# Two gates of a linear recurrence: from two 128-row products to pairs of 64-row tiles of the matmul array

## The chip, the cores and the metric

The kernel runs as one program on one core of one Trainium2 chip. The metric is the device time of one execution in microseconds (us). The core has five engines that run side by side and wait for each other by semaphores: PE (TensorE, matmuls), DVE (VectorE), ACT (ScalarE), POOL (GpSimd) and SP (SyncE, which here issues most DMAs).

## The reference

The program is one decoder block on 512 tokens of width 1024. A first norm and a wide projection feed a pooling mixer and a gated linear recurrence; both are merged by sigmoid gates, projected out, normed again and sent through a mixture of 16 experts, two per token. What matters here is the recurrence:

```python
xc = conv(u) + conv_b                                  # causal, 4 taps, per channel
xh = xc.reshape(b_, s_, LRU_HEADS, LRU_HEAD_DIM)       # 16 heads of 64 channels
r = sigmoid(einsum('bshc,hcd->bshd', xh, w_r) + b_r)   # a 64x64 matrix per head
i = sigmoid(einsum('bshc,hcd->bshd', xh, w_i) + b_i)   # another 64x64 matrix per head
log_a = -RG_C * r * softplus(-lam)
a = exp(log_a)
bt = sqrt(-expm1(2.0 * log_a)) * (i * xc)
h[t] = a[t] * h[t-1] + bt[t]                           # along the 512 tokens
y_b = (h * gelu(gate_in)) @ proj_b
```

## The kernel before, in words

Activations lie feature-major: 128 channels on the partitions, 512 tokens along a row. A block `c` of 128 channels, of which there are 8, so holds two heads. Products are computed to near float32 precision by splitting each operand into a high and a low part of type float32r; one product is then three matmuls (high by high, high by low, low by high: `mm3`, lines 241 to 244). Weights arrive in chunks of 1 MB (`raw`), and each half of a chunk is split by one ACT cast (line 151, `w` high) and one DVE subtraction (line 152, `w` low). The program calls them `w6_0`, `w6_1` and so on: chunk 6, first and second half.

The stages around the change follow each other on PE:

- **Recurrence input**: for each `c` a product of 24 matmuls (`zl`), an ACT and three DVE instructions for the convolution (`xc`, lines 286 to 289), and its split `xcp` (ACT line 291, DVE line 292). The gates of block `c` are computed two blocks later: `lru_gates` (line 295) multiplies `xcp` by two matrices of 128x128, each of which holds the 64x64 matrices of two heads on its diagonal and zeros beside them, into the PSUM banks `pr` and `pi`. ACT evicts each bank with one sigmoid (lines 300 and 302) and goes on with a tanh (304) and an exp (307).
- **Pooling input** (`zp`, 4 products), with running sums on DVE (`pn`, `pz`) and a split `zp`; the last two gate blocks are computed here.
- **Gate input** (`zg`, 8 products, from chunks 6 to 9). Beside it ACT and DVE do the rest of the recurrence: square, sqrt, products, eight scans (line 317), gelu and the splits `yh` and `yl`.
- **Merge** (`zga` and `ya`), and all that follows.

Three things set the order of the work. The instructions of each engine stand in a fixed order, which a scheduler chose when the program was built from its own estimate of when each would be ready; a scheduler's choice can so put a weight split early or late among other work. Tiles come from pools with a fixed number of buffers (`b8`: 20 buffers of 16 KB a partition, `s4`: 6 of 4 KB a partition, PSUM: 8 banks), and who takes a buffer waits until it is free. Weight loads are issued in one order on SP's queue, at most three in flight. ACT evaluates some functions only with the right table loaded (`ACT_TABLE_LOAD`): sigmoid and exp as they are used here need different ones.

The block-diagonal matrices are built at the start: DVE clears `bd_raw` (line 199), four DMAs write the 64x64 matrices, and one ACT cast and one DVE subtraction of 2048 elements a partition split it into `bd0` and `bd1`.

Of the kernel before, what the change touches and what calls it, by code (L numbers as in the profile page):

```python
# [8 lines left out]
F32 = mybir.dt.float32  # L9
F32R = mybir.dt.float32r  # L10
# [3 lines left out]
AF = mybir.ActivationFunctionType  # L14
# [3 lines left out]
P = 128  # L18
S = 512
D = 1024  # L20
KD = D // P
# [15 lines left out]
def tile_hybrid_block(  # L37
# [7 lines left out]
    PE, ACT, DVE, POOL, SP = nc.tensor, nc.scalar, nc.vector, nc.gpsimd, nc.sync  # L45
# [7 lines left out]
    const = ctx.enter_context(tc.tile_pool(name="const", bufs=1))  # L53
# [3 lines left out]
    def b8(shape, dtype, name):  # L57
        return sb.tile(shape, dtype, tag="b8", name=name, bufs=20)

    def s4(shape, dtype, name):  # L60
        return sb.tile(shape, dtype, tag="s4", name=name, bufs=6)
# [4 lines left out]
    def bank(name):  # L66
        return psum.tile([P, 512], F32, tag="ps", name=name)
# [4 lines left out]
    class Feat:  # L72
        """[P, KD, S] in two tiles."""

# [19 lines left out]

# [1 line left out]
    chunks = []  # L96
# [36 lines left out]
    raws, pairs, loads = {}, {}, {}  # L133
# [16 lines left out]
    def split(r, hi, lo):  # L150
        ACT.copy(hi, r)  # L151
        DVE.tensor_tensor(lo, r, hi.bitcast(F32), op=ALU.subtract)  # L152
# [17 lines left out]

# [1 line left out]
    x_rows = [s4([P, D], F32, f"x_rows{t}") for t in range(NT)]  # L172
# [7 lines left out]

# [1 line left out]
    ident = const.tile([P, P], F32, name="ident")  # L182
# [10 lines left out]
    for nm, ap, n in vecs:  # L193
# [3 lines left out]
        r0 += n  # L197
    bd_raw = b8([P, 2, KD, P], F32, "bd_raw")
    DVE.memset(bd_raw, 0.0)
    for j, w in enumerate((rg_w_r, rg_w_i)):  # L200
        wv = w.rearrange("(c two) k m -> two k c m", two=2)
        for two in range(2):
            half = slice(64 * two, 64 * two + 64)
            SP.dma_start(bd_raw[half, j, :, half], wv[two])
    load_raw(2)
    g1, lam, cb, br, bi, psc, g2f = (par[n] for n in ("g1", "lam", "cb", "br", "bi", "psc", "g2f"))
    cw = par["cw"].rearrange("p (j c) -> p j c", j=4)

# [1 line left out]
    def rstd_of(src, name):  # L210
# [30 lines left out]
    def mm3(acc, whi, wlo, mhi, mlo, first, last):  # L241
        PE.matmul(acc, whi, mhi, start=first, stop=False)
        PE.matmul(acc, whi, mlo, start=False, stop=False)
        PE.matmul(acc, wlo, mhi, start=False, stop=last)
# [7 lines left out]

# [1 line left out]
    sp8 = const.tile([P, KD], F32, name="sp8")  # L254
# [24 lines left out]

# [1 line left out]
    ra, ix, uu = Lazy(F32, "ra"), Lazy(F32, "ix"), Lazy(F32, "uu")  # L281
    bd = []

    def lru_conv(c, ps):
# [8 lines left out]
        return c, xc, xp  # L293

    def lru_gates(c, xc, xp):
        pr = bank(f"pr{c}")
        mm3(pr, bd[0][:, 0, c, :], bd[1][:, 0, c, :], xp[:, 0], xp[:, 1], True, True)
        pi = bank(f"pi{c}")
        mm3(pi, bd[0][:, 1, c, :], bd[1][:, 1, c, :], xp[:, 0], xp[:, 1], True, True)
        ACT.activation(ra[c], pr, AF.Sigmoid, bias=br[:, c:c + 1])  # L300
        it = s2([P, S], F32, f"it{c}")
        ACT.activation(it, pi, AF.Sigmoid, bias=bi[:, c:c + 1])
        DVE.tensor_tensor(ix[c], it, xc, op=ALU.mult)
        ACT.activation(uu[c], ra[c], AF.Tanh, scale=sp8[:, c:c + 1])
# [9 lines left out]
    def lru_scan(c):  # L314
        ACT.activation(uu[c], uu[c], AF.Sqrt)
        DVE.tensor_tensor(ix[c], uu[c], ix[c], op=ALU.mult)
        DVE.tensor_tensor_scan(uu[c], ra[c], ix[c], 0.0, op0=ALU.mult, op1=ALU.add)

    pend = []
    for c in range(KD):  # L320
        wp = weights(c_lru[c // 2], 2, 3)
        ps = feat_block(wp, (c % 2) * P, KD, xh, xl, f"zl{c}")
        if c == 0:
            with tc.issue_after(xl_last):
                softplus()
            bd += [b8([P, 2, KD, P], F32R, f"bd{i}") for i in range(2)]
            split(bd_raw, *bd)
        if len(pend) == 2:
            lru_gates(*pend.pop(0))
        pend.append(lru_conv(c, ps))  # L330

# [1 line left out]
    icnt = const.tile([P, PAD], F32, name="icnt")  # L333
# [74 lines left out]

# [1 line left out]
    m = Lazy(F32, "m")  # L410
# [17 lines left out]

# [1 line left out]
    NR = 2 * NG + NE  # L430
# [53 lines left out]
    rows = const.tile([P, NE], I32, name="rows")  # L484
# [13 lines left out]

# [1 line left out]
    x2s, h2s, xts, xpart, xg = {}, {}, {}, [], []  # L500
# [160 lines left out]
    for t in range(NT):  # L661
# [4 lines left out]
        for n in range(2):  # L666
            po = bank(f"po{t}_{n}")
            for kh in range(2):
                w = weights(c_wo[n][kh], 2 if n + kh < 2 else 0, RA[2 * t + n])
                for kk in range(4):  # L670
# [6 lines left out]
                    if kk % 2 == 1:  # L677
# [3 lines left out]
                        if step == 5 and t == NT - 1:  # L681
                            xg.append(s4([P, D], F32, "xg0"))
                            POOL.memset(xg[0], 0.0)
                            first = gather(rows0, xg[0], (NT - 1) * P)
# [95 lines left out]

# [1 line left out]
    cn = bank("cn")  # L782
# [8 lines left out]
    for e in range(NE):  # L791
        pg = bank(f"pg{e}")
# [25 lines left out]

# [1 line left out]
    n_max = nc.values_load(nmi[0:1, 0:1], min_val=0, max_val=S)  # L820
# [54 lines left out]

# [1 line left out]
    xb = [b8([P, 2, D], F32, f"xb{i}") for i in range(2)]  # L877
# [73 lines left out]
```

## Time and profile before

| | |
|---|---|
| time, median of 3 runs | 697.42 us (696.87 to 699.47) |
| span of the profiled execution, first to last instruction | 695.7 us |
| median less that span | 1.7 us |
| busy: PE, DVE, ACT | 650.9, 502.5, 431.4 us |

The profiler gives the profiled execution's span and no separate time for it, so the 1.7 us by which the median of the runs exceeds the span stand for what lies around it and for the difference between executions. Matmuls are pipelined: a matmul's row lasts 0.39 us, but the next one starts 0.23 us after it, so PE reads as busy all the time when they follow each other without a gap. A wait is printed at the end of a row, in brackets, as idle time of the engine and what ended it.

### The profile page before, as it was taken

What the parts mean: (1) busy time and instruction counts of PE and PEld (TensorE: products, weight loads), DVE (VectorE), ACT (ScalarE), POOL (GpSimd) and SP (SyncE); (2) the same over time, 40 slices, a digit from 0 to 9 for tenths busy, and PEclk for the clock granted to TensorE, in tenths of its full rate; (3) what the DMA queues carried; (4) which work ended last, traced back from release to release, by engine and by line L of the source; (5) the groups of instructions that cost most, each with busy time, mean ns of one, the idle gap of its engine ahead of it and who ended that gap; (6) DMA issues with size and microseconds to landing.
All of it is one profiled execution on the core that took longest, in us unless ns stands there. A gap on an engine that the chain in (4) does not pass through costs nothing. (4 is left out here: it accounts for less than half of the span.)

```text
span 695.7 us, 8405 instructions
## 1 busy us (share of the span) xinstructions
PE 650.9 (94%) x3044; PEld 526.8 (76%) x3044; DVE 502.5 (72%) x792; ACT 431.4 (62%) x579; POOL 79.6 (11%) x101
## 2 busy tenths in 40 slices
PE   5999999999999999999959999999999999999970
PEld 4888888788888888887747787777777777777850
DVE  6886699952322227556687898898899888887946
ACT  6599957752213225141244888888888888777913
POOL 3000000000100000000131111111111111101013
PEclk9999999999999999999988999999999999999996
DMA  7920323213217113696584999999999999999134
GB/s 215 345 79 20 127 81 118 95 62 122 65 62 241 53 69 121 235 389 236 198 310 134 334 333 342 341 351 338 331 337 336 361 336 342 335 339 365 53 98 161
DMA packets 88053, 153.23 MB, mean 220 GB/s; under 512 B 7250, under 2 KB 29894, under 8 KB 88009
## 3 DMA queue, kind: packets, MB, share of 16 engines
q1 hardware_dynamic: 81736, 138.98, 57.5%
q0 software_dynamic: 5824, 12.64, 6.8%
q10 hardware_dynamic: 448, 1.05, 0.4%
q8 instruction: 24, 0.39, 0.2%
q14 instruction: 21, 0.16, 0.1%
HBM read 146.67 MB, written 14.16 MB: 231 GB/s over the span
## 5 line engine op out<-in xcount | busy, mean ns | idle before, releaser
L152 DVE TENSOR_TENSOR w<-raw,w 128x1024 fp32r<-128x1024 f32 x248 | 293.6, 1220 | 69.7 <-ACT w L151 67.6
L151 ACT CAST w<-raw 128x1024 fp32r<-128x1024 f32 x248 | 249.7, 1051 | 59.4 <-DVE w L152 14.1
L727 PE MATMUL pu<-w,xt 128*128 128x512 f32 x128 | 51.9, 406 | 2.3 <-DVE w L152 2.3
L726 PE MATMUL pu<-w,xt 128*128 128x512 f32 x128 | 52.2, 408 | 1.8 <-ACT w L151 1.8
L726 PE MATMUL pg<-w,xt 128*128 128x512 f32 x128 | 52.8, 412 | 1.1
L727 PE MATMUL py<-w,ht 128*128 128x512 f32 x128 | 51.6, 403 | 0.0
L728 PE MATMUL py<-w,ht 128*128 128x512 f32 x128 | 50.7, 396 | 0.6 <-DVE ht L505 0.6
L728 PE MATMUL pg<-w,xt 128*128 128x512 f32 x128 | 50.4, 394 | 0.5 <-DVE xt L505 0.5
L728 PE MATMUL pu<-w,xt 128*128 128x512 f32 x128 | 50.7, 396 | 0.0
L727 PE MATMUL pg<-w,xt 128*128 128x512 f32 x128 | 50.3, 393 | 0.3 <-DVE w L152 0.3
L508 POOL DMA_INDIRECT xg<-h_rows,rows x16 | 26.9, 1679 | 197.6 <-PE xtp L718 177.8
L726 PE MATMUL py<-w,ht 128*128 128x512 f32 x128 | 48.8, 395 | 0.8 <-ACT ht L504 0.8
L743 POOL DMA_INDIRECT x_acc<-y,rows x15 | 24.6, 1639 | 62.9 <-ACT y L774 36.4
L727 PEld LDWEIGHTS pu<-w,xt 128*128 128x128 f32 x128 | 24.5, 191 | 8.8 <-DVE w L152 3.2
L726 PEld LDWEIGHTS pg<-w,xt 128*128 128x128 f32 x128 | 24.1, 188 | 9.4 <-ACT w L151 5.3
L726 PEld LDWEIGHTS pu<-w,xt 128*128 128x128 f32 x128 | 24.3, 190 | 7.7 <-ACT w L151 3.1
L726 PEld LDWEIGHTS py<-w,ht 128*128 128x128 f32 x128 | 24.5, 191 | 6.1 <-ACT ht L504 1.0
L505 DVE TENSOR_TENSOR xt<-xtp,xt 128x512 fp32r<-128x512 f32 x30 | 19.4, 686 | 13.4 <-ACT xt L504 13.4
L727 PEld LDWEIGHTS pg<-w,xt 128*128 128x128 f32 x128 | 24.1, 188 | 6.2 <-DVE w L152 0.7
L728 PEld LDWEIGHTS py<-w,ht 128*128 128x128 f32 x128 | 24.4, 191 | 5.7 <-DVE ht L505 1.0
L728 PEld LDWEIGHTS pg<-w,xt 128*128 128x128 f32 x128 | 24.0, 188 | 5.8 <-DVE xt L505 1.1
L728 PEld LDWEIGHTS pu<-w,xt 128*128 128x128 f32 x128 | 24.5, 191 | 4.8
(292 smaller groups left out, 1414.6 us busy)
## 6 DMA issues: line engine op xcount, KB each, us to landing
raw<-in_exp_w_gate_dram SPq DMA_DIRECT2D x32, 1024.0 KB, 8.0
raw<-in_exp_w_up_dram SPq DMA_DIRECT2D x32, 1024.0 KB, 7.9
raw<-in_exp_w_down_dram SPq DMA_DIRECT2D x32, 1024.0 KB, 10.7
raw<-in_w_in_dram SPq DMA_DIRECT2D x17, 1024.0 KB, 7.7
raw<-in_proj_b_dram SPq DMA_DIRECT2D x4, 1024.0 KB, 9.3
raw<-in_w_out_dram SPq DMA_DIRECT2D x4, 1024.0 KB
x_rows<-in_x_dram SPq DMA_DIRECT2D x4, 512.0 KB
xrow<-in_x_dram SPq DMA_DIRECT2D x4, 512.0 KB
```

What stands on the lines that cost most here:

```text
L151: ACT.copy(hi, r)
L152: DVE.tensor_tensor(lo, r, hi.bitcast(F32), op=ALU.subtract)
L505: DVE.tensor_tensor(lo, tv, hi.bitcast(F32), op=ALU.subtract)
L508: return POOL.indirect_dma_start(out=dst, out_offset=None, in_=h2d[:n, :], in_offset=bass.IndirectOffsetOnAxis(ap=idx, axis=0), bounds_che ...
L726: PE.matmul(ps, hi, w[:, 0, k % 2, :], start=first and k == 0, stop=False)
L727: PE.matmul(ps, hi, w[:, 1, k % 2, :], start=False, stop=False)
L728: PE.matmul(ps, lo, w[:, 0, k % 2, :], start=False, stop=last and k == 3)
L743: POOL.indirect_dma_start(out=xd, out_offset=bass.IndirectOffsetOnAxis(ap=idx, axis=0), in_=src, in_offset=None, bounds_check=S - 1, oob_i ...
```

## The change

For each head, `r` and `i` matrices now stand side by side as one matrix of 64 rows and 128 columns. The two heads of a block use the two halves of the array's rows: rows 0 to 63 write to one PSUM bank (`pg0`), rows 64 to 127 to another (`pg1`). The number of matmul instructions per block stays six (three parts for each of two heads), each with 64 rows in place of 128. In one bank lie `r` of a head and `i` of the same head in different partition halves, and the second head has the halves exchanged, so that `r` always stands in the partitions where it is used; `i` is moved to the other half by its eviction. Each sigmoid so becomes two of 64 partitions. The raw matrices lose their zeros and half their size: they move from pool `b8` to pool `s4`, the clearing goes, the split shrinks from 2048 to 1024 elements a partition, and both parts share one buffer. Two small copies build a bias with exchanged halves (`bisw`).

```diff
-    bd_raw = b8([P, 2, KD, P], F32, "bd_raw")
-    DVE.memset(bd_raw, 0.0)
+    bd_raw = s4([P, KD, P], F32, "bd_raw")
     for j, w in enumerate((rg_w_r, rg_w_i)):
         wv = w.rearrange("(c two) k m -> two k c m", two=2)
         for two in range(2):
-            half = slice(64 * two, 64 * two + 64)
-            SP.dma_start(bd_raw[half, j, :, half], wv[two])
+            jj = j ^ two
+            SP.dma_start(bd_raw[64 * two:64 * two + 64, :, 64 * jj:64 * jj + 64], wv[two])
...
+    HALVES = (slice(0, 64), slice(64, P))
+
     def lru_gates(c, xc, xp):
-        pr = bank(f"pr{c}")
-        mm3(pr, bd[0][:, 0, c, :], bd[1][:, 0, c, :], xp[:, 0], xp[:, 1], True, True)
-        pi = bank(f"pi{c}")
-        mm3(pi, bd[0][:, 1, c, :], bd[1][:, 1, c, :], xp[:, 0], xp[:, 1], True, True)
-        ACT.activation(ra[c], pr, AF.Sigmoid, bias=br[:, c:c + 1])
+        pg = [bank(f"pg{c}_{j}") for j in range(2)]
+        for w, m in ((0, 0), (0, 1), (1, 0)):
+            for j, h in enumerate(HALVES):
+                PE.matmul(pg[j], bd[w][h, c, :], xp[h, m], start=w + m == 0, stop=w == 1)
         it = s2([P, S], F32, f"it{c}")
-        ACT.activation(it, pi, AF.Sigmoid, bias=bi[:, c:c + 1])
+        for j, h in enumerate(HALVES):
+            o = HALVES[1 - j]
+            ACT.activation(ra[c][h], pg[j][h], AF.Sigmoid, bias=br[h, c:c + 1])
+            ACT.activation(it[h], pg[j][o], AF.Sigmoid, bias=bisw[o, c:c + 1])
         DVE.tensor_tensor(ix[c], it, xc, op=ALU.mult)
...
-            bd += [b8([P, 2, KD, P], F32R, f"bd{i}") for i in range(2)]
+            bdp = b8([P, 2, KD, P], F32R, "bdp")
+            bd += [bdp[:, i] for i in range(2)]
             split(bd_raw, *bd)
+            for h, o in ((HALVES[0], HALVES[1]), (HALVES[1], HALVES[0])):
+                DVE.tensor_copy(bisw[h], bi[o])
```

The scheduler moves other work in answer. PE's order stays as it was apart from the gate matmuls themselves, and so does the order of SP and of POOL. ACT and DVE change between the first recurrence block and the middle of the gate input; before and behind that they keep their order.

ACT, gates of blocks 2 and 3, before (`pr`, `pi`: gate banks; `nsp8`: the exp's scale; `sp8`: the tanh's):

```order
L307 ACT_TABLE_LOAD
L307 ACTIVATE ra0_372<-ra0_372,nsp8_214 128x512 x2
L300 ACT_TABLE_LOAD
L300 ACTIVATE ra0_372<-pr2_467,vec_90 128x512
L291 CAST xcp3_431<-xc3_426 128x512
L302 ACTIVATE it2_476<-pi2_471,vec_90 128x512
L304 ACTIVATE uu0_378<-ra0_372,sp8_213 128x512
L286 ACTIVATE xc4_480<-zl4_442,vec_90 128x512
L307 ACT_TABLE_LOAD
L307 ACTIVATE ra0_372<-ra0_372,nsp8_214 128x512
L300 ACT_TABLE_LOAD
L300 ACTIVATE ra0_372<-pr3_513,vec_90 128x512
```

ACT at the same place in the changed program, from the cast of `xcp3` on:

```order
L290 CAST xcp3_436<-xc3_431 128x512
L305 ACT_TABLE_LOAD
L305 ACTIVATE ra0_374<-pg2_0_472,vec_90 64x512
L306 ACTIVATE it2_480<-pg2_0_472,bisw_214 64x512
L305 ACTIVATE ra0_374<-pg2_1_473,vec_90 64x512
L306 ACTIVATE it2_480<-pg2_1_473,bisw_214 64x512
L308 ACTIVATE uu0_381<-ra0_374,sp8_212 128x512
L285 ACTIVATE xc4_487<-zl4_447,vec_90 128x512
L305 ACTIVATE ra0_374<-pg3_0_520,vec_90 64x512
L306 ACTIVATE it3_528<-pg3_0_520,bisw_214 64x512
L305 ACTIVATE ra0_374<-pg3_1_521,vec_90 64x512
L306 ACTIVATE it3_528<-pg3_1_521,bisw_214 64x512
```

Each block now has four sigmoids in place of two, and two blocks stand behind one table load where each had its own, because fewer exps are put between them. From the cast of `xcp1` to the copy `pu1` of the second pooling block ACT had 12 table loads, 16 sigmoids and 7 exps; it now has 7 table loads, 32 half sigmoids and 4 exps, and the same casts, copies, convolutions and tanhs.

DVE, second and third pooling group, before (`pn`, `pz`: running sums; `zp1`: the low part of the second group's split; `w7`: the weights of the gate input's second chunk):

```order
L361 TENSOR_TENSOR phead_1_767<-pn1_2_763,icnt_637 128x3
L152 TENSOR_TENSOR w7_0_875<-raw7_540,w7_0_875 128x1024
L362 TENSOR_TENSOR pz1_765<-phead_1_767,pu1_758 128x3
L152 TENSOR_TENSOR w7_1_878<-raw7_540,w7_1_878 128x1024
L365 TENSOR_TENSOR zp1_770<-pz1_765,zp1_770 128x512
L355 TENSOR_TENSOR pn2_1_809<-pu2_806 128x527
L355 TENSOR_TENSOR pn2_2_811<-pn2_1_809 128x525
L355 TENSOR_TENSOR pn2_4_813<-pn2_2_811 128x521
```

DVE at the same place in the changed program:

```order
L369 TENSOR_TENSOR phead_1_784<-pn1_2_780,icnt_650 128x3
L370 TENSOR_TENSOR pz1_782<-phead_1_784,pu1_775 128x3
L373 TENSOR_TENSOR zp1_787<-pz1_782,zp1_787 128x512
L363 TENSOR_TENSOR pn2_1_826<-pu2_823 128x527
L363 TENSOR_TENSOR pn2_2_828<-pn2_1_826 128x525
L363 TENSOR_TENSOR pn2_4_830<-pn2_2_828 128x521
L152 TENSOR_TENSOR w7_0_892<-raw7_549,w7_0_892 128x1024
L367 SCALAR_TENSOR_TENSOR pz2_832<-pn2_4_830,pu2_823 128x512
L369 TENSOR_TENSOR phead_2_834<-pn2_4_830,icnt_650 128x7
L152 TENSOR_TENSOR w7_1_895<-raw7_549,w7_1_895 128x1024
```

The two splits of `w7` stood ahead of `zp1` and now stand behind it. From `zp1` to the split `w9_0` of the gate input's last chunk DVE's queue holds these two more and otherwise the same instructions, some of them in another order.

## Rows read from the trace of the kernel before

**Rows 1.** The page's first line.

```profile
span 695.7 us, 8405 instructions
```

**Rows 2.** Chain of gate matmuls, PE timeline: start, us, engine, line, operation, out<-in.

```profile
33.47 0.39 PE L242 MATMUL pr<-xcp,bd 128*128 128x512 f32 x1
...
34.83 0.39 PE L242 MATMUL zl<-xh,w 128*128 128x512 f32 x1
```

**Rows 3.** One of six groups of gate matmuls, by tile: duration min/median/max, starts.

```profile
L242 PE MATMUL pr<-xcp,bd x8: 388/389/389, 33.5 to 81.1; 128*128 128x512 f32 x8
```

**Rows 4.** PE timeline around a 64-row product of the router (L556, L557).

```profile
312.32 0.39 PE L676 MATMUL po<-w,mt 128*128 128x512 f32 x1
312.63 0.40 PE L556 MATMUL lgt<-sel,ls 64*128 64x24 f32 x2
...
313.19 0.50 PE L674 MATMUL po<-w,mt 128*128 128x512 f32 x1
313.52 0.39 PE L675 MATMUL po<-w,mt 128*128 128x512 f32 x1
```

**Rows 5.** Busy time by stretch: length, PE, PEld, DVE, ACT, POOL, clock, DMA, GB/s.

```profile
40.00:60.00 20.00, 20.00 (x90) 16.53 (x90) 14.34 (x20) 19.86 (x27) 0.00 (x0) 1.00 0.16 54
60.00:80.00 20.00, 20.00 (x90) 16.57 (x89) 13.30 (x17) 19.84 (x25) 1.04 (x3) 1.00 0.20 66
100.00:120.00 20.00, 20.00 (x90) 16.44 (x89) 19.72 (x28) 17.33 (x26) 0.54 (x1) 1.00 0.30 95
120.00:140.00 20.00, 18.27 (x81) 14.82 (x80) 19.65 (x27) 14.52 (x20) 0.00 (x0) 1.00 0.35 116
140.00:160.00 20.00, 20.00 (x90) 16.57 (x89) 11.58 (x13) 9.99 (x12) 0.00 (x0) 1.00 0.15 54
```

**Rows 6.** PE timeline, the wait in the gate input.

```profile
131.40 0.50 PE L244 MATMUL zg<-xh,w 128*128 128x512 f32 x1 [1.73 <-DVE w L152]
```

**Rows 7.** DVE timeline, from the second pooling group to that wait.

```profile
91.59 1.22 DVE L152 TENSOR_TENSOR w<-raw,w 128x1024 fp32r<-128x1024 f32 x1
92.73 0.69 DVE L365 TENSOR_TENSOR zp<-pz,zp 128x512 fp32r<-128x512 f32 x1
...
97.20 0.69 DVE L365 TENSOR_TENSOR zp<-pz,zp 128x512 fp32r<-128x512 f32 x1 [0.68 <-ACT zp L364]
...
130.12 2.35 DVE L152 TENSOR_TENSOR w<-raw,w 128x1024 fp32r<-128x1024 f32 x2
```

**Rows 8.** ACT timeline, first gate block and second pooling group.

```profile
35.15 0.62 ACT L291 CAST xcp<-xc 128x512 fp32r<-128x512 f32 x1 [5.37 <-DVE sacc L272]
...
37.09 0.69 ACT L300 ACTIVATE ra<-pr,vec 128x512 f32<-128x512 f32 x1
37.67 0.68 ACT L302 ACTIVATE it<-pi,vec 128x512 f32<-128x512 f32 x1
...
87.43 0.58 ACT L348 COPY pu<-zp 128x512 f32<-128x512 f32 x1
```

**Rows 9.** ACT groups from 30 to 140 us: busy, mean ns, idle before.

```profile
L300 ACT ACT_TABLE_LOAD x6 | 7.7, 1283 | 0.1
...
L307 ACT ACTIVATE ra<-ra,nsp 128x512 f32<-128x512 f32 x8 | 5.7, 722 | 0.1
...
L348 ACT COPY pu<-zp 128x512 f32<-128x512 f32 x4 | 2.3, 581 | 0.0
```

**Rows 10.** An ACT copy of half the partitions (router, L553).

```profile
L553 ACT COPY ls<-lg x3: 365/366/367, 310.3 to 343.1; 64x256 f32<-64x256 f32 x3
```

**Rows 11.** The split of the gate matrices, DVE.

```profile
L152 DVE TENSOR_TENSOR bd<-bd_raw,bd x1: 2283/2283/2283, 27.4 to 27.4; 128x2048 fp32r<-128x2048 f32 x1
```

**Rows 12.** Two later stretches, columns as in rows 5.

```profile
358.00:363.00 5.00, 0.69 (x9) 0.63 (x10) 4.96 (x8) 1.31 (x2) 2.97 (x2) 0.71 1.03 385
623.00:627.00 4.00, 4.00 (x12) 3.12 (x11) 3.41 (x3) 3.04 (x3) 0.00 (x0) 0.58 1.06 337
```

**Rows 13.** Waits of SP's queue: in all, times, longest.

```profile
SPq L143 <- PE po L676: 20.4, 5, 9.9
```

More of the change, by code (lines that the diff above doesn't have):

```diff
@@ L317, in lru_scan @@
         DVE.tensor_tensor_scan(uu[c], ra[c], ix[c], 0.0, op0=ALU.mult, op1=ALU.add)
+    bisw = const.tile([P, KD], F32, name="bisw")
     pend = []
```

## The prediction

> **What bounds the kernel now.** I read the busy times by stretch first, then the idle times printed in the timelines of PE, DVE and ACT. From 40 to 80 us, where the gates are computed, PE is busy 20.00 of 20 us and ACT 19.86 and 19.84 [rows 5]: PE is the bound, and ACT has nothing to spare. From 100 to 140 us DVE is the full one, 19.72 and 19.65 of 20 [rows 5], and there PE has its only wait of the whole front part: at 131.40 us, idle for 1.73 us until DVE has split `w9_0`, weights of the gate input's last chunk [rows 6]. That split starts at 130.12, in a DVE queue that has run from `zp1` at 92.73 with one longer hole, 0.68 us at 97.20 [rows 7]. From 140 us on PE is full again and DVE and ACT half empty [rows 5]. So the reader is to see a relay: PE sets the pace to about 129 us, then DVE hands `w9_0` over late, and then PE sets the pace once more. A microsecond that PE saves before 129 us is worth nothing unless `w9_0` comes sooner as well; a microsecond by which `w9_0` comes later is paid in full. What is late or early at 140 us is taken through to the end: the later weight loads wait for buffers that matmuls free (SP's queue waits for `po`, for one, five times, 20.4 us) [rows 13].
>
> **PE's part.** A block's six gate matmuls take from 33.47 to 34.83, 1.36 us, 0.227 each [rows 2]; there are 48 of them, six groups of eight [rows 3], 10.9 us. If the two heads of a pair run side by side, a block takes three such steps, 0.68 us, and 8 blocks save 5.4 us; if they run one behind the other, nothing. No row shows two row halves at work at once, so both ends stand. I take the side-by-side value, since the two matmuls of a pair read different rows and write different banks. Going to 64 rows and back has a row, though: around the router's 64-row product the step into it is 0.31 us (312.32 to 312.63) and the first step behind it 0.33 (313.19 to 313.52) [rows 4], against 0.227; 0.08 and 0.10 more, 0.19 a block, 1.5 us for 8. PE's gain is then 5.4 - 1.5 = 3.9 us, between -1.5 and 5.4.
>
> The Trainium skill speaks on both ends. By "TensorE: Matmul & The Clock Gate", section "Part 3: Packing small matmuls — row/col tiling", matmuls in distinct row groups run concurrently; no run here shows it yet, and by it the 5.4 us stand. By "TensorEngine Tiling (Array Packing)", section "Tiling Modes", changing the tiling mode drains TensorE; rows 4 agree that a change costs, 0.08 to 0.10 us each way. If a drain were the whole rest of a matmul, 0.389 - 0.227 = 0.16 us, 16 changes would cost 2.6 us and PE's gain would be 2.8.
>
> **ACT's part.** A sigmoid of 64 partitions costs what one of 128 does: a copy of 64x256 takes 366 ns [rows 10] and one of 128x512 581 [rows 9], so a row's length of 256 more costs 215 ns, 0.84 ns an element, which leaves about 150 ns for either, whatever the partitions. Sigmoids follow each other by 37.67 - 37.09 = 0.58 us [rows 8]. Between the cast of `xcp1` at 35.15 and the copy `pu1` at 87.43 [rows 8] the changed queue has 16 more sigmoids, +9.3 us; 5 fewer table loads of 1.28 [rows 9], -6.4; 3 fewer exps of 0.72 less 0.1 overlap [rows 9], -1.9. Sum: +1.0 us. ACT is full there [rows 5], so this counts. The start comes earlier: ACT waits 5.37 us for DVE before `xcp1` [rows 8], and DVE's queue ahead of that loses half of the 2.28 us split [rows 11], -1.1, and gains two copies of 8 columns, about 0.15 each, +0.3. So `pu1` comes at 87.43 + 1.0 - 0.8 = 87.6. The removed clearing lies in the first microseconds, while DVE waits for the input, and is worth nothing; the `b8` buffers set free let loads start sooner that nobody waits for (DMA moves only 54 and 66 GB/s there [rows 5]).
>
> **DVE's part, on which the end rests.** In the changed queue the running sums behind `pu1` need not wait for the two `w7` splits: copy 0.6, two sums and `pz1` 2.1, the fix of its head 0.3 give 90.6; ACT's cast follows behind a table load and two exps (87.6 + 0.5 + 1.3 + 1.2 = 90.6) and takes 0.6; DVE starts `zp1` at about 91.5, against 92.73 [rows 7], 1.2 us sooner. But the `w7` splits now stand behind it, at 92.73 - 91.59 = 1.14 us each [rows 7], 2.3 us, in the stretch where DVE is full. Everything else from there to `w9_0` is the same work. `w9_0` is ready 2.3 - 1.2 = 1.1 us later than before. Bounds: if `zp1` starts when it did, 2.3 later; if the hole of 0.68 us closes and PE's earlier products draw ACT forward by another 1.7, 1.3 us earlier.
>
> **The sum.** PE gets to `w9_0` 3.9 us sooner and leaves it 1.1 us later; the gain turns into a wait there (and part of it at the chunk before, whose splits come later by the same). What the path gets is +1.1 us: the median of 697.42 becomes 698.5, or on the profiled execution, 695.7 [rows 1] + 1.1 = 696.8 us of span plus the 1.7 us by which the median stands above it. Own range 696.1 to 699.7. The Trainium skill has this in general: by "TensorEngine Tiling (Array Packing)", section "Performance Considerations", tiling speeds up TensorE but not PSUM evacuation; rows 5 agree, with ACT at 19.8 of 20 us.
>
> **The rivals.**
>
> *The wait brings the slower clock.* PE's waits in the gate input would add up to 1.7 + 3.9 + 1.1 = 6.7 us, close to each other. In the stretch 358 to 363 us, where PE is busy 0.69 of 5 us, the granted clock falls from its full 2.4 to a mean of 0.71 of it [rows 12], that is, to 1.2 GHz for part of it; at 623 to 627, a stretch at 0.58, 12 matmuls start in 4.00 us where 17.6 would at 0.227 [rows 12], 5.6 lost, 1.3 us. Against it: the present wait of 1.73 us left the clock at 1.00 [rows 5]. Time: 698.5 + 1.3 = 699.8 for one such stretch, 701.1 for two.
>
> *The halves don't run side by side (slower).* If they run one behind the other and the weights of a pair are not loaded ahead, each matmul takes its whole 0.389 us [rows 3] in place of 0.227: 6 x 0.16 + 0.19 = 1.16 us more a block, 9.3 us. PE has 1.7 us to spare at `w9_0` [rows 6], and 1.1 more by DVE's lateness; ACT would not be late for it. From 2.8 us on, 0.35 a block, PE decides, and 9.3 - 1.7 = 7.6 us are paid: 705.0. If they only run one behind the other at 0.227, the price is the 1.5 us of the switches, under the 2.8, and nothing shows in the end. For it: no row has such a pair. Against it: different rows, different banks.
>
> *DVE comes early (faster).* If `zp1` starts as much sooner as PE is ahead, 3.9 us, and ACT lets it, `w9_0` comes 3.9 - 2.3 = 1.6 us sooner, and with the hole closed 2.3; were the splits of `w7` then also hidden, all 3.9 to 5.4 us would come through: 693.5 to 692.0. Against it: ACT has 1.0 us more to do, not less, and stood at 19.8 of 20.
>
> **How the numbers follow.** My forecast 47%, the slower clock on top 33%, one behind the other 13%, DVE early 7%. The likeliest gives 698.5. Its own range and the clock's (697.4 to 701.0 for one stretch) are taken in, with half a microsecond below and 1.0 above for a second stretch and the difference between executions (three runs lay between 696.87 and 699.47): 695.6 to 702.0, which leaves out the last two rivals' ends. About 0.5%, 3.5 us, is what a measurement can tell from no change. Slower by more (over 700.9): 0.12 from the second rival and a quarter of the clock's, 0.20 in all. Faster by more (under 693.9): 0.06. The same: 0.74.
>
> **What would show it.** Right: six gate matmuls in about 0.9 us from the first of a block to the next `zl`; half sigmoids 0.58 us apart; ACT full from 40 to 88 us; PE idle before `zg` matmuls for 5 us or more in all, ended by `w` L152 or L151; the first `zga` about 1.1 us later than before. Wrong: a block of 1.4 us or more (second rival); fewer than 3 us of PE waits in the gate input and the first `zga` 2 us or more sooner than before (third); a stretch of the clock below 1.00 between 120 and 145 us (first). Wrong in its ground would be a loss or gain that arises behind 150 us, where both programs have the same order.

## The result, and the profile after

The changed kernel takes 705.38 us (median of four runs, 703.18 to 707.09) against 697.9 for the kernel before (median of four): a ratio of 1.0114, 95% interval 1.0092 to 1.0137. It is slower by 7.5 us, outside the range forecast. In the profiled execution the span grew by 7.8 us, and 7.4 of them are there before the merge begins: the first `zga` stands at 149.40 us in place of 141.96.

The page's first line of the kernel after, against [rows 1]:

```profile
span 703.5 us, 8424 instructions
```

The PE timeline after (start, us, engine, line, operation, out<-in; idle before and what ended it): the first gate block, against [rows 2], the wait for a later block, the waits in the gate input, against [rows 6], and the first merge matmul.

```profile
33.25 0.39 PE L243 MATMUL zl<-xh,w 128*128 128x512 f32 x1
33.57 0.96 PE L301 MATMUL pg<-xcp,bdp 64*128 64x512 f32 x6
34.46 0.50 PE L241 MATMUL zl<-xh,w 128*128 128x512 f32 x1
34.80 0.40 PE L242 MATMUL zl<-xl,w 128*128 128x512 f32 x1
...
61.80 0.50 PE L301 MATMUL pg<-xcp,bdp 64*128 64x512 f32 x2 [1.94 <-ACT xcp L290]
...
133.72 0.50 PE L241 MATMUL zg<-xh,w 128*128 128x512 f32 x1 [2.11 <-ACT w L151]
...
136.14 0.80 PE L243 MATMUL zg<-xh,w 128*128 128x512 f32 x1 [1.69 <-DVE w L152]
...
149.40 0.39 PE L241 MATMUL zga<-xh,w 128*128 128x512 f32 x1
```

The row halves do run side by side: six matmuls take from 33.57 to 34.46, 0.89 us, where they took 1.36 [rows 2]. But TensorE now waits 1.94 us for a cast on ACT in the gate stage, where it had no wait, and twice in the gate input, 3.8 us against 1.73 [rows 6].

Busy time by stretch after (columns as in [rows 5], whose stretches the rows from 40 us answer):

```profile
40.00:60.00 20.00, 19.86 (x91) 14.74 (x90) 14.17 (x18) 19.67 (x27) 0.00 (x0) 1.00 0.10 33
60.00:80.00 20.00, 17.98 (x75) 13.20 (x76) 13.14 (x18) 19.70 (x27) 0.97 (x3) 0.91 0.20 66
...
100.00:120.00 20.00, 20.00 (x89) 16.46 (x88) 19.18 (x31) 14.99 (x24) 0.00 (x0) 1.00 0.23 80
120.00:140.00 20.00, 16.05 (x61) 12.22 (x60) 19.72 (x26) 16.41 (x23) 0.54 (x1) 0.88 0.27 93
140.00:160.00 20.00, 20.00 (x85) 16.43 (x85) 12.08 (x13) 10.67 (x14) 0.00 (x0) 0.95 0.29 91
...
62.00:67.00 5.00, 4.78 (x16) 3.28 (x15) 3.40 (x5) 4.94 (x7) 0.00 (x0) 0.66 0.00 0
135.00:142.00 7.00, 5.86 (x14) 4.65 (x15) 6.66 (x9) 6.07 (x9) 0.00 (x0) 0.51 0.45 147
```

ACT is as full as it was, since there is always more for it to do. What is new is the granted clock: 0.66 from 62 to 67 us, behind the wait for the cast, and 0.51 from 135 to 142, behind those of the gate input. Both are 1.00 before.

The ACT timeline after: the first block's four sigmoids, a half sigmoid behind a whole activation, the late cast, and `pu1`, against [rows 8]; and the cast of `w9_0`.

```profile
36.96 0.68 ACT L305 ACTIVATE ra<-pg,vec 64x512 f32<-64x512 f32 x1
37.66 0.69 ACT L306 ACTIVATE it<-pg,bisw 64x512 f32<-64x512 f32 x1
38.37 0.69 ACT L305 ACTIVATE ra<-pg,vec 64x512 f32<-64x512 f32 x1
39.08 0.68 ACT L306 ACTIVATE it<-pg,bisw 64x512 f32<-64x512 f32 x1
39.78 0.78 ACT L285 ACTIVATE xc<-zl,vec 128x512 f32<-128x512 f32 x1
...
57.04 0.76 ACT L285 ACTIVATE xc<-zl,vec 128x512 f32<-128x512 f32 x1
57.70 0.68 ACT L305 ACTIVATE ra<-pg,vec 64x512 f32<-64x512 f32 x1
...
61.15 0.60 ACT L290 CAST xcp<-xc 128x512 fp32r<-128x512 f32 x1
...
91.92 0.56 ACT L356 COPY pu<-zp 128x512 f32<-128x512 f32 x1
...
132.63 1.04 ACT L151 CAST w<-raw 128x1024 fp32r<-128x1024 f32 x1
```

Each half lasts as long as a whole one, but the next starts 0.70 to 0.71 us later, behind its end; whole ones follow each other by 0.58 [rows 8], a tenth before the end of the one ahead. The half at 57.70 does start a tenth before the end of the whole activation ahead of it; more on that under e5. And `pu1` comes at 91.92, 4.5 us later.

What DVE waits for between 34 and 100 us: first before, then after (waited for, us in total, times, longest).

```profile
DVE xcp L292 <- ACT xcp L291: 8.9, 5, 2.2
...
DVE ix L303 <- ACT it L302: 1.9, 1, 1.9
```

```profile
DVE ix L307 <- ACT it L306: 14.2, 8, 3.4
DVE xc L287 <- ACT xc L285: 2.2, 3, 0.7
```

All in all 15.8 us of such waits became 19.6, and they changed place: DVE's queue now stands still at each block's product `ix`, eight times, for the last of four half sigmoids. `zp1` and the splits of `w9` further on in that queue, against [rows 7]:

```profile
95.78 0.69 DVE L373 TENSOR_TENSOR zp<-pz,zp 128x512 fp32r<-128x512 f32 x1 [0.69 <-ACT zp L372]
...
134.88 1.21 DVE L152 TENSOR_TENSOR w<-raw,w 128x1024 fp32r<-128x1024 f32 x1
...
136.62 1.21 DVE L152 TENSOR_TENSOR w<-raw,w 128x1024 fp32r<-128x1024 f32 x1
```

The loss is then two terms. `w9_0` is split from 134.88 instead of 130.12 on, 4.76 us later. From that split to the first `zga` it takes 14.52 us instead of 11.84, 2.68 more, the stretch at half clock lying there. Together 7.44, the delay of `zga`. The wait and the slow clock near 62 us cost nothing on their own, since TensorE has to wait for `w9_0` in any case (e1, below, has no wait there, and its split comes as late). ACT's cast of `w9_0` ended at 133.67, only 1.2 us ahead of DVE's split, and the first of TensorE's two waits is for it; a DVE early by more than that would have found the cast late.

### The profile page after: what moved, and what is told of

It is laid out like the page before. It is cut to its first block, busy times and chain, and to the rows that moved or that the text cites. A ratio compares the mean times of both kernels' runs of the same rounds, so it can differ in the third digit from the quotient of the medians.

```text
span 703.5 us, 8424 instructions
## 1 busy us (share of the span) xinstructions
PE 653.8 (93%) x3044; PEld 523.5 (74%) x3044; DVE 501.2 (71%) x793; ACT 440.9 (63%) x593; POOL 79.6 (11%) x101
## 5 line engine op out<-in xcount | busy, mean ns | idle before, releaser
L735 PEld LDWEIGHTS pu<-w,xt 128*128 128x128 f32 x128 | 24.4, 190 | 8.7 <-DVE w L152 3.2
L734 PEld LDWEIGHTS pu<-w,xt 128*128 128x128 f32 x128 | 24.4, 191 | 7.8 <-ACT w L151 3.1
L513 DVE TENSOR_TENSOR xt<-xtp,xt 128x512 fp32r<-128x512 f32 x30 | 19.4, 686 | 13.5 <-ACT xt L512 12.7
L243 PE MATMUL zg<-xh,w 128*128 128x512 f32 x64 | 26.4, 413 | 1.8 <-DVE w L152 1.7
```

Of the source, the lines that this page charges most:

```text
L513: DVE.tensor_tensor(lo, tv, hi.bitcast(F32), op=ALU.subtract)
L734: PE.matmul(ps, hi, w[:, 0, k % 2, :], start=first and k == 0, stop=False)
L735: PE.matmul(ps, hi, w[:, 1, k % 2, :], start=False, stop=False)
```

## The experiments

Theory A: the 32 half sigmoids make ACT late, and with it DVE and `w9_0`. Rivals: the pairs on TensorE; the exchange between partitions; the new order of the splits on DVE.

A table of all runs. The split, the work and the waits are read from the profile of each: the start of `w9_0`'s split, DVE's busy time up to there, and the rest of that time. A profile is of one execution, up to 2.1 us from the median of its run; a ratio is to runs of the kernel before taken beside it.

```
                    split   DVE work  DVE waits  first zga  time us  ratio to before (95%)
before              130.12  104.3     25.8       141.96     697.9    1
after               134.88  102.8     32.1       149.40     705.4    1.0114 (1.0092-1.0137)
e1 halves, old prod 135.13  105.2     29.9       148.57     703.9    1.0066 (1.0039-1.0094)
e2 pairs, whole     129.52  102.0     27.6       142.94     697.1    0.9998 (0.9972-1.0024)
e3 exps last        133.01  102.9     30.1       147.21     702.5    1.0057 (1.0032-1.0082)
e4 before+exps last 126.82  104.8     22.0       138.86     694.5    0.9944 (0.9919-0.9968)
e5 by input         140.05  103.2     36.8       153.12     707.1    one run
e6 pool first       137.03  102.7     34.3       150.17     704.8    1.0109 (1.0067-1.0152)
e7 three reliefs    135.02  102.9     32.2       146.85     700.8    1.0032 (1.0006-1.0058)
e8 exchange on DVE  131.42  112.0     19.4       144.87     700.1    1.0031 (1.0008-1.0054)
e9 exps+conv        125.42  102.2     23.2       137.24     693.5    0.9947 (0.9928-0.9965)
e10 exch. on GpSimd 134.39  107.3     27.1       146.22     701.0    1.0042 (1.0023-1.0061)
e12 e10+adds        137.06  102.6     34.5       150.36     707.7    1.0141 (1.0117-1.0166)
e13 before+exps+cv  127.79  103.8     24.0       139.82     694.2    0.9948 (0.9927-0.9969)
e14 conv only       136.03  102.5     33.5       149.27     704.1    1.0100 (1.0076-1.0124)
e15 e8+conv         133.03  111.7     21.3       144.90     699.3    1.0021 (1.0006-1.0037)
e16 late products   132.70  102.4     30.3       144.54     700.4    1.0038 (1.0015-1.0061)
```

### One part of the change at a time: e1, e2

```
e1, before:  for h in halves:  ACT.activation(ra[c][h], pr[h], Sigmoid, ...)
                               ACT.activation(it[h], pi[h], Sigmoid, ...)
e2, after:   ACT.activation(ra[c], pg[0], Sigmoid, ...)
             ACT.activation(it, pg[1], Sigmoid, ...)
```

> The kernel before with its two 128x128 block-diagonal products kept, but each product evicted by partition halves (four sigmoids a block, none crossing partitions). Theory A (ScalarE: 32 half sigmoids 0.70 us apart for 16 whole ones 0.58 apart fill ScalarE, its casts come late, TensorE waits): 704 to 709 us, a wait of 1.5 us or more on ScalarE at a gate product near 60 us, sigmoids about 0.70 apart. Rival B (the halves cost only because r and i change partitions, or because of the paired products, or the new order of the splits): 697 to 700 us, as before, halves 0.58 apart.

> The changed kernel with its 64-row pairs, but each of the two banks evicted by one sigmoid of 128 partitions (it leaves out the exchange of r and i between the halves, so half of the gates belong to the wrong place). Theory A: no wait on ScalarE near 60 us, 695 to 698 us, that is 0 to 3 us under the kernel before (eight blocks 0.27 us shorter each, less what the wait at the ninth weight chunk takes back). Rival (the pairs, their switches or the changed loads at the start cost the time, not the eviction): 703 us or more.

e1 lost most of what the change lost: 703.9 us, just under the range of theory A, the split at 135.13. By the medians that is 6.2 of 7.5 us, by the ratios 0.66 of 1.14 per cent. The halves alone, with the old products and no crossing of partitions, are enough for that; its wait near 60 us stayed away (0.37 us at 83.7), so that part of the expectation missed. e2 came to 697.1, level with before: pairs, switches and loads cost nothing. Nor did they gain, since `w9_0` is where it was and TensorE waits for its cast on ACT and then for its split:

```profile
129.38 0.50 PE L241 MATMUL zg<-xh,w 128*128 128x512 f32 x1 [2.27 <-ACT w L151]
...
130.79 0.73 PE L243 MATMUL zg<-xh,w 128*128 128x512 f32 x1 [0.67 <-DVE w L152]
```

That is the step of the prediction by which TensorE's gain turns into a wait; it held. The first `zga` of e2 came 1.0 us later than before, with the slower clock behind the split, and its time is level all the same.

### Why 0.70 us: e5

```
-r(pg0,0:64) it(pg0,64:128) r(pg1,64:128) it(pg1,0:64)
+r(pg0,0:64) it(pg1,0:64)   r(pg1,64:128) it(pg0,64:128)     (bank, partitions read)
```

> The changed kernel with the four sigmoids of a block in another order: both that read partitions 0 to 63 first, then both that read 64 to 127. Theory I (an activation starts 0.1 us before the end of the one before it only where both read the same partitions): starts 0.58, 0.70, 0.58 us apart. Theory O (only where both write the same partitions): 0.70, 0.58, 0.70. Theory IO (only where both read and write the same ones): 0.70 throughout, as in the changed kernel. The time: 702 to 706 us in each case, since at most 1.9 us of ScalarE come back.

The ACT timelines of e1 and of e5, one block of each:

```profile
54.30 0.68 ACT L302 ACTIVATE ra<-pr,vec 64x512 f32<-64x512 f32 x1
54.88 0.67 ACT L303 ACTIVATE it<-pi,vec 64x512 f32<-64x512 f32 x1
55.57 0.69 ACT L302 ACTIVATE ra<-pr,vec 64x512 f32<-64x512 f32 x1
56.16 0.67 ACT L303 ACTIVATE it<-pi,vec 64x512 f32<-64x512 f32 x1
```

```profile
37.60 0.68 ACT L307 ACTIVATE ra<-pg,vec 64x512 f32<-64x512 f32 x1
38.30 0.68 ACT L309 ACTIVATE it<-pg,bisw 64x512 f32<-64x512 f32 x1
38.99 0.68 ACT L307 ACTIVATE ra<-pg,vec 64x512 f32<-64x512 f32 x1
39.70 0.68 ACT L309 ACTIVATE it<-pg,bisw 64x512 f32<-64x512 f32 x1
```

In e1, `ra` and `it` of one half read and write the same partitions and follow by 0.58 and 0.59; from one half to the other it is 0.69. In e5, where two neighbours share either the partitions they read or those they write, it is 0.70 throughout: theory IO. In the changed kernel no two neighbours share both. Rows beside whole activations narrow this down. A half from partition 0 starts 0.1 us before the end of a whole activation (57.70 in the changed kernel), and a whole cast 0.58 us behind a half from partition 0 (e1, at 44.52). A half from partition 64 starts 0.65 us behind a whole cast of 0.62, so behind its end (changed kernel, cast at 44.38). What has to agree is then the partition at which both begin to read and to write, not all of their partitions. The time of e5, 707.1 us in its one run, lies above the expected 702 to 706; why stays open. The Trainium skill, "ScalarE: Activation LUTs", section "What ACT_TABLE_LOAD costs", says that activations back to back overlap by about 93 ns; whole ones do here (0.69 long, 0.58 apart), halves that begin at different partitions do not.

### Relieving ACT: e3, e4, e6, e7

```
e3, e4:  with tc.issue_after(last_tanh):  lru_decay(c)     (after; before)
e6:      pool_pre(g, ps) ahead of lru_gates(...)           (after)
e7:      e3 + e5 + e6
```

> The changed kernel with its eight exps of the decay held behind the last tanh, so that ScalarE loads no table for them between the sigmoids: six loads of 1.28 us fewer between 40 and 92 us. Theory A (ScalarE's total is what is late): the wait near 60 us goes and 4 to 6 us of the 7.5 lost come back, 699 to 702 us, first merge matmul near 144 to 146 us. Rival C (the order of the splits on VectorE makes the ninth chunk late, whatever ScalarE does): the first wait goes, but the first merge matmul stays within 1.5 us of 149.4 us, 704 us or more.

> The kernel before with the same hold on its exps (ten table loads fewer between 40 and 92 us). Theory A: ScalarE held nothing up there in this kernel, so 695 to 699 us, no change that can be measured. Rival (table loads of ScalarE were already on the path in the kernel before, and 12.8 us fewer of them bring a gain): 694 us or less.

> The changed kernel with the pooling mixer's PSUM copy (pu) written ahead of the gates of the same step, so that ScalarE copies pu1 ahead of the last eight half sigmoids. Theory A (VectorE has 42 to 43 us of work from pu1 to the ninth chunk's first split, so the late pu1 makes that split late): pu1 at 86 to 88 us, the ninth split 2.5 to 5 us sooner than 134.9, the time 700 to 703 us. Rival C (the order of the splits on VectorE, or the late ScalarE cast of the ninth chunk, sets it): split within 1.5 us of 134.9 us, 704 to 707 us.

> The changed kernel with three reliefs of ScalarE together: exps behind the last tanh, pu ahead of the gates, the half sigmoids ordered by the partitions that they read. Theory A (ScalarE's lateness is all that the change lost): first merge matmul at 140 to 143 us, 695 to 699 us, level with the kernel before its own relief. Rival (something else in the pairs or in VectorE's order costs): 701 us or more.

By the medians e3 gave back 2.9 us: less than theory A wanted, but the first `zga` came 2.2 us sooner, which the rival excluded. e4 was a surprise: the kernel before gains 3.2 us (693.56 once more, ratio 0.9938, 0.9915 to 0.9962), as the rival had it in kind. Its DVE had waited 25.8 us before the split, and 22.0 now; the split comes 3.3 us sooner and the 1.73 us wait [rows 6] is gone. TensorE is busy without a gap from 30 to 145 us there (115.00 of 115.00 us), so it sets the first `zga` itself. So ACT's table loads were on the path already in the kernel before. e6 missed both expectations of the split: `pu1` came sooner (90.15) and the split later, 137.03; `pu1` alone does not set it. e7 fell between both expectations in time, and its first `zga`, 146.85, is far from theory A's 140 to 143; it holds e5's order too, so its parts cannot be told apart.

> The kernel before with its exps behind the last tanh, once more, beside e10 and e12 on one chip: 693.5 to 695.5 us, 0.4 to 0.7 per cent under the kernel before, as at first.

### What e6 and e7 teach: the split is DVE's work plus its waits

The rows of the table that stretch from 0 to the split (third busy time: DVE), of before, after and e9:

```profile
0.00:130.12 130.12, 121.05 (x528) 99.85 (x528) 104.34 (x173) 102.71 (x141) 7.88 (x45) 0.99 0.43 136
```

```profile
0.00:134.88 134.88, 121.13 (x528) 94.62 (x528) 102.77 (x174) 110.61 (x154) 7.83 (x45) 0.99 0.41 131
```

```profile
0.00:125.42 125.42, 115.82 (x525) 91.60 (x526) 102.21 (x174) 100.62 (x147) 7.89 (x45) 1.00 0.45 143
```

In all kernels that leave the exchange to ACT, DVE has 102 to 105 us of work before that split, and the split comes when this is done plus whatever DVE waited on the way, wherever that was. That the two columns add up is by the way they are made; what they teach is that the work hardly differs, so that the waits decide. Behind the split the first `zga` follows in 11.8 to 12.0 us where the clock stays at 1.00 from there on (before, e4, e7, e9, e10, e13, e15, e16) and in 13.1 to 14.5 where a stretch of the slower clock lies between (the others, 0.76 to 0.87 on average). In e4 and e13 that is not the split's doing, since TensorE is busy without a gap there. From the first `zga` to the last instruction all profiles take 551.4 to 555.4 us, so a difference of under 4 us between two runs cannot be laid to the split by its profile alone.

### The exchange elsewhere: e8, e10, e12, e15

```
ACT.activation(ra[c], pg[0], ...); ACT.activation(it, pg[1], ...)      # whole
e8:   DVE.tensor_tensor(ix[c][h], (ra[c], it)[j][other half], xc[h], mult), two halves
      DVE.tensor_copy(ra[c][64:128], it[64:128])
e10:  three POOL.tensor_copy of a half in their place
e12:  e10 + POOL.tensor_tensor for the mixer's second and further adds
e15:  e8 + e9's order
```

> Pairs on TensorE as in the changed kernel, but each bank evicted by one whole sigmoid, and the exchange of the halves done on VectorE: two half products in place of one whole one, and a half copy of r (about 1 us more a block on VectorE, 8 us in all, in the stretch where it is 13 to 15 us of 20 busy), with the exps behind the last tanh. Theory A (ScalarE's halves are the whole loss, and the 2.1 us of the eight shorter blocks are real): no wait near 60 us, 691 to 695 us, 0 to 3 us under the kernel before with its exps held (694.5 us). Rival (VectorE becomes late, at the ninth split or at an xcp): 696 to 700 us.

> Pairs on TensorE, each bank evicted by one whole sigmoid, the exchange of the halves by three half copies a block on GpSimd (idle there), exps behind the last tanh. ScalarE and VectorE then have the work of e4_before_exps_last (694.5 us). Theory A2: VectorE waits for ScalarE 10 to 12 us between 34 and 100 us, the ninth split at 126 to 128 us as there; the eight blocks, 0.27 us shorter each, bring TensorE to that split 2.1 us sooner, and since VectorE is busy without a gap from 101 us up to it, that becomes a wait of 1 to 2 us: 693.5 to 697 us, no gain over e4. Rival (the pairs' 2.1 us are a gain once ScalarE is relieved): 691.5 to 693 us. Another (GpSimd's copies are late or slow VectorE): over 698 us.

> As e10_whole_pool, and the pooling mixer's second and further adds (six of 128x512, 0.7 us each on VectorE) moved to GpSimd (1.3 us each by the nearest row, a product of 128x512 at the end). Theory A2: 4 us of VectorE's unbroken work before the ninth split go, the split comes 2 to 4 us sooner, no wait there, and the pairs' 2.1 us show: 690.5 to 693.5 us, under e4. Rival (GpSimd's adds lie on the chain to zp and make the mixer late instead, or VectorE slows beside GpSimd): 695 us or more.

> e8_whole_dve (pairs, whole sigmoids, the exchange of the halves on VectorE; 700.1 us) with the convolution written ahead of the gates. Theory A3: VectorE has 8 to 9 us more work than in e9 before the ninth split and hardly waits for ScalarE in e8 already (0.7 us from 34 to 60), so the order helps little: 698 to 700 us. Rival (order is all): 692 to 695 us.

The rival was right in e8: DVE hardly waits any more (19.4 us), but works 112.0. e15 is the same by its order, as expected. e10 and e12 lost, as the last rival of each had it, and in two ways. DVE now waits for GpSimd (from 34 us to the split): in e10 for the copies, in e12 for them, 4.7 us, and for the adds.

```profile
DVE ix L311 <- POOL it L309: 3.6, 4, 1.2
```

```profile
DVE pz L372 <- POOL pn L368: 6.9, 3, 3.7
```

And DVE's operations are longer while GpSimd copies. DVE timeline of e10:

```profile
43.41 1.23 DVE L152 TENSOR_TENSOR w<-raw,w 128x1024 fp32r<-128x1024 f32 x1 [0.76 <-ACT w L151]
...
46.41 1.04 DVE L291 TENSOR_TENSOR xcp<-xc,xcp 128x512 fp32r<-128x512 f32 x1
47.38 1.62 DVE L152 TENSOR_TENSOR w<-raw,w 128x1024 fp32r<-128x1024 f32 x1
...
53.99 0.69 DVE L291 TENSOR_TENSOR xcp<-xc,xcp 128x512 fp32r<-128x512 f32 x1 [0.74 <-ACT xcp L290]
```

Here a split takes 1.62 us beside GpSimd's copies (45.93 to 49.5) and 1.23 without, a subtraction 1.04 and 0.69. The Trainium skill, "SBUF — State Buffer", section "SBUF: two separate sides", has GpSimd and VectorE contend for a shared port pair where VectorE reads two SBUF inputs; these rows agree that the two hinder each other, and show no more.

### Sum or order: e9, e13, e14, e16

```
 for c in range(KD):
+    pend.append(lru_conv(c, ps))
-    if len(pend) == 2:  lru_gates(*pend.pop(0))
-    pend.append(lru_conv(c, ps))
+    if len(pend) == 3:  lru_gates(*pend.pop(0))
e9: after, with e3's hold;  e13: before, with it;  e14: after, without it
e16: e3 + product ix held behind the convolution two steps on (issue_after)
```

> The changed kernel with its exps behind the last tanh (as in e3_exps_last, 702.5 us) and with each step's convolution written ahead of the gates of the block two steps back, so that more of the casts xcp stand ahead of half sigmoids on ScalarE. Theory A2 (what sets the first merge matmul is how long VectorE waits for ScalarE between 34 and 100 us, 16.4 us in e3 and 15.7 in the kernel before): those waits fall to 13 to 15 us, the ninth split to 130 us, 698 to 700 us. Rival (the order on ScalarE does not matter, only its sum): 701 to 704 us as e3.

> The kernel before with the two edits of e9_conv_first (exps behind the last tanh, each step's convolution written ahead of the gates). Theory A3 (the halves cost nothing once ScalarE's casts stand ahead of the sigmoids, so the pairs' 8 times 0.27 us are what e9 has over this one): 694.5 to 696.5 us, 1 to 3 us over e9. Rival (the order alone made e9 fast, and whole sigmoids under it gain more still than the pairs): 692 us or less, under e9.

> The changed kernel with the convolution written ahead of the gates and nothing else (exps between the sigmoids as the scheduler puts them, three loads of a table there and back). Theory A3 (the order of casts and sigmoids on ScalarE is the larger part of the loss, the table loads the smaller): VectorE waits for ScalarE 14 to 17 us between 34 and 100 us, 696 to 700 us, most of the loss of 7.5 us back. Rival A (the sum of ScalarE's work is what counts, and the two reliefs are needed together): 702 to 705 us.

> e3_exps_last (the changed kernel with exps behind the last tanh, 702.5 us, 32 half sigmoids), with the product ix of each gate block held on VectorE behind the convolution two steps on, so that VectorE's queue does not stand still for the block's last half sigmoid (9.2 of its 16.4 us of waits for ScalarE between 34 and 100 us in e3). Theory W (that standing still at ix is what the halves cost, since the convolution of the next steps and its cast queue up behind it): waits at ix under 3 us, ninth split at 126 to 129 us, 693 to 697 us. Rival A (the halves' sum on ScalarE is the price, the waits only move from ix to xcp and xc): VectorE's waits for ScalarE 15 us or more as before, 700 to 703 us.

> e9_conv_first once more, beside e13 on one chip: 692.5 to 694.5 us, 0.4 to 0.7 per cent under the kernel before.

e9 went past its expectation: 693.5 us, and 692.87 once more (0.9928, 0.9912 to 0.9944), with the same 32 half sigmoids. What DVE waits for from 34 to 100 us in e9, and in e16:

```profile
DVE w L152 <- ACT w L151: 3.9, 5, 1.0
...
DVE ix L309 <- ACT it L308: 1.8, 5, 0.4
```

```profile
DVE xc L295 <- ACT xc L293: 11.9, 6, 2.8
DVE xcp L299 <- ACT xcp L298: 3.3, 5, 0.7
...
DVE ix L289 <- ACT it L316: 0.6, 2, 0.4
```

In e9 the 14.2 us at `ix` (9.2 in e3) are 1.8, and the waits sum to 12.0. In e16 the wait at `ix` was taken away by force, and it went to `xc` (2.9 us in e3, 11.9 here), 17.9 us of waits in all against 16.4 in e3: rival A was right in its mechanism, with 700.4 us at the edge of its range. DVE's place of waiting is not the cause; ACT's lateness is. e14 shows that the order alone gains nothing that can be measured (704.1, as rival A had it): with the exps among the sigmoids, ACT is full, and whatever goes first delays the rest. Its busy times by stretch:

```profile
40.00:60.00 20.00, 20.00 (x93) 15.03 (x92) 13.74 (x23) 19.66 (x27) 0.00 (x0) 1.00 0.16 54
60.00:80.00 20.00, 20.00 (x93) 14.99 (x93) 10.21 (x15) 19.57 (x27) 0.97 (x3) 1.00 0.20 66
```

So the two reliefs are worth far more together, 11.9 us by the medians, than apart, 2.9 (e3) and 1.3 (e14, within the intervals). As I read the queues, six fewer loads make room on ACT, and the order puts what DVE needs next into it. e13, the kernel before with both, came to 694.2: whole sigmoids gain nothing from the order over e4 (694.5, 693.6), where TensorE had no wait left to lose. e9's medians lie 0.7 to 1.3 us under e13's, on the side of the pairs' 2.1 us, but the intervals overlap; whether the pairs gain in the end is not settled. The traces point to a gain: e9's TensorE reaches the first `zga` at 137.24 us (138.49 once more), that of e4 and e13, without a wait in both profiles, at 138.86 and 139.82 (e4 once more 139.15). e9 is the fastest of all by its medians, 0.5 to 0.7 per cent under the kernel before.

## Why the prediction was wrong

- **TensorE's part: right in kind, half in size.** The halves run side by side, as said. The gain was put at 0.49 us a block. The price of the switches was right: the step into the block is 0.32 us (0.09 more) and the step behind it 0.34 (0.11 more), 0.20 a block where 0.19 was put. Mis-sized was the block itself: from its first matmul to the next `zl` it takes 0.89 us, 0.21 more than three steps of 0.227. So a block gains 1.36 - 0.89 - 0.09 - 0.11 = 0.27, 2.1 us for eight instead of 3.9. The sign "about 0.9 us" was met, but by another sum: the working had 0.68 for the six, and its 0.19 lay in the steps beside them. It did not matter, since the gain was a wait in the end, as said.
- **ACT's part: the step that failed.** "Sigmoids follow each other by 0.58 us" was carried from whole ones to halves. They follow by 0.70, so 32 of them take 22.5 us where 16 took 9.3: 13.2 more, not 9.3. The loads and exps held, five and three fewer ahead of `pu1` (counted in both timelines: 12 and 7, 7 and 4). The earlier start did not: the cast of `xcp1` came at 35.02, 0.1 us sooner than in [rows 8] where 0.8 was put. With 3.9 us more `pu1` comes at 91.5 instead of 87.6, with the start's 0.7 at 92.2; measured 91.92.
- **DVE's part: the chain held, its input did not.** The forecast had `w9_0` later by 1.1 us with `pu1` 0.2 later; with 4.5 it would have said 5.4; measured 4.8. `zp1` starts 3.9 us behind `pu1`, as in the working; from there to `w9_0` it is 39.1 us against 37.4 [rows 7], so the two splits of `w7` cost 1.7 us where 2.3 was put. But e6 shows that following `pu1` alone was too narrow: every wait of DVE for ACT from 34 us on counts, and the change added 3.8 us of them. Up to the split its waits grew by 6.3 us and its work fell by 1.6; 1.9 of the waits lie ahead of 34 us, where the clearing and half of the gate matrices' split are gone, 3.9 from there to 100 and 0.5 behind it.
- **The first rival came true on top of it.** A stretch of the slower clock lies between 135 and 142 us, where it was looked for, given 33%. It was priced at 1.3 us; it cost 2.68. With the sigmoids at 0.70 and this price the working gives 698.5 + 3.9 + 2.7 = 705.1; measured 705.4. That it comes so close is in part luck: the start's 0.7 us and the 0.6 put too much on the splits cancel. The second rival's 705.0 is as near by luck alone, since the halves do not run one behind the other.
- **The other rivals** fell: the halves run side by side, and DVE was not early. TensorE's idle time before `zg` was 3.8 us, under the 5 forecast; 1.94 had been spent near 60 us, the slower clock there made it late, and its own gain was smaller. Nothing arose behind 150 us but 0.4 us. One reading was too wide: the wait at 131.40 us is TensorE's only one from 34 us on, but of the first 34 us it is idle for 8.6.

## What to carry to other kernels

Before an eviction is cut into pieces, price the piece by the distance between two starts, not by the length or by the distance of its whole sibling, and look at whether the evicting engine is full there. A split deep in a queue comes when that engine's work and all its waits are over, so count every wait ahead of it, not the last one. Where an engine is full, first take table loads out from between the work, then put ahead what the next engine waits for: together they turned a loss of 7.5 us into a gain of 4 to 5.

## What was not expected of the hardware

- In all rows looked at here, an activation of 64 partitions starts 0.1 us before the end of its neighbour only if both begin at the same partition where they read and where they write: 0.58 against 0.69 to 0.71 us between starts of half sigmoids (e1, e5, after).
- A split on VectorE took up to 1.62 us instead of 1.23, and a subtraction 1.04 instead of 0.69, beside GpSimd's half copies (e10).
- A block of three row pairs among 128-row matmuls costs 0.41 us more than three steps of 0.227: 0.09 in the step into it, 0.21 within it, 0.11 in the step behind it (after).
- Waits of like length left the granted clock differently: the 1.94 us near 60 us were followed by a granted clock of 0.66 from 62 to 67 us, the 1.73 us at 131 us before left it at 1.00.
